# Row sums of ReLU on one core: the second load takes another 8 MB block in a different deal of rows to partitions, and the 15-row block comes third

## The chip, the core and the metric

The kernel runs on one core of a Trainium2 chip. The input lies in HBM, the chip's memory; DMA engines, 16 for the core, move it into SBUF, the core's working memory of 128 partitions. ScalarE (ACT) and VectorE (DVE) compute there; SyncE (SP) issues every DMA of this kernel. The metric is the device time of one execution in microseconds. Before the change the median of three runs is 161.04 us (160.92 to 161.04).

## The reference

```python
batch, seq, dim = 32, 512, 1024
x = randn(batch, seq, dim)          # float32, 64 MB

def reference(x):
    relu_x = np.maximum(x, 0)
    return np.sum(relu_x, axis=-1).astype(np.float32)
```

There are 16,384 rows of 1,024 numbers (4 KB each). Of each row the positive numbers are added up. The output is 64 KB.

## The kernel before

The input is seen as 16,384 rows. The first 2,048 rows, 8 MB, form block 0, and every further 2,048 rows another block: blocks 0 to 6 and a last one that is cut into smaller loads. A block holds 16 rows for each of the 128 partitions. There are three buffers `io0` to `io2` of 8 MB (`bufs`), used in turn.

*Which row lies where.* Block 0 is split. Its first 128 rows, one for each partition, are a load of their own of 512 KB (`ahead`), so that VectorE has something to add early. The other 1,920 rows are `xf`: 15 adjacent rows, 60 KB, for each partition. All later blocks are slices of `xv`, which gives each partition one long run of adjacent rows of the remaining input; of these a block takes 16 for each partition. The results lie in one SBUF tensor `res`, a column for each row of a partition (128 columns); column 0 stays unused, since the sums of the first 128 rows go through `one` and `turned`.

*The order of the loads.* The loop over j (lines 160 to 195) issues one 8 MB load per block, from SyncE, all on one queue. Load 0 is preceded by `ahead`. The first three have a buffer each and wait for nothing. A later one waits (`freed`) until VectorE has finished with the block that held its buffer three loads before. Counted with `ahead` the order of transfers is thus: 512 KB, then the 15-row load, then 16-row loads. The last 8 MB come as 8 rows, 4 rows and the last four rows in four unequal loads (lines 198 to 233), so that little work is left after the last byte.

*The work on a block.* `TWO[j]` lists how many rows one pair of instructions takes: ScalarE clamps them at zero in place (`clamp`, line 121), then VectorE adds up each row (`total`, line 129). `ACT[j]` and `DVE[j]` rows are done by a single instruction on one engine, which clamps and adds together (`act_row`, line 136; `dve_row`, line 144). The first three blocks are one pair of instructions each.

*The stores.* After all loads have been issued, SyncE issues the stores of the results (lines 237 to 240): columns 1 to 15 in two halves of 64 partitions, the first 128 sums, then columns 16 to 125 in one store that waits for nearly the last sum. The last two columns are stored at the very end (line 255).

Of the kernel before, what the change touches and what calls it, by code (L numbers as in the profile page):

```python
# [7 lines left out]
P = 128  # L8

ROWS = 16  # L10
NBUF = 3


TWO = [[15], [16], [16], [8, 8], [8, 8], [7, 7], []]
ACT = [0, 0, 0, 0, 0, 2, 9]
DVE = [0, 0, 0, 0, 0, 0, 7]

# [9 lines left out]
def kernel(tc: tile.TileContext, x: bass.AP, out: bass.AP):  # L27
    nc = tc.nc
    sems = Semaphores(tc)

    tc.close()
    tc.compile()
    nc.cur_bb = nc.bb_map[tc.start_bb_name]
    body = nc.cur_bb.bb.instructions
    ends = list(body)
    body.clear()
    n_stores = relu_sum(nc, sems, x, out)
    body.extend(ends)


    nc.cur_bb = nc.bb_map[tc.start_bb_name + "_end"]
    nc.cur_bb.bb.instructions.clear()
    nums = sorted(s.num for s in (*sems.loads, sems.act, sems.dve))
    cleared = range(nums[0], nums[-1] + 1)
    assert len(cleared) == len(nums)
    nc.sync.sem_clear(cleared)
    nc.sync.wait_ge(sems.stored, 16 * n_stores).then_inc(sems.stored, -16 * n_stores)
    open_without_barrier(tc, EARLY)


class Semaphores:
    def __init__(self, tc: tile.TileContext):
        n = 1 + len(TWO) + len(TAIL) + 2 + len(PIECES)
        self.loads = [tc.alloc_semaphore(f"load{i}") for i in range(n)]
        self.act = tc.alloc_semaphore("act")
        self.dve = tc.alloc_semaphore("dve")
        self.stored = tc.alloc_semaphore("stored")


def relu_sum(nc, sems: Semaphores, x: bass.AP, out: bass.AP):  # L60
    x_flat = x.flatten_outer_dims()
    N, D = x_flat.shape
    NT = N // P
    NB = len(TWO)
    assert N == P * NT == P * ROWS * (NB + 1)
    assert sum(TAIL) == ROWS - 4 and START_PIECE + END_PIECE + sum(PIECES) == D

    bufs = [nc.alloc_sbuf_tensor(f"io{i}", [P, ROWS, D], F32) for i in range(NBUF)]
    res = nc.alloc_sbuf_tensor("res", [P, NT], F32)
# [8 lines left out]
    one = nc.alloc_sbuf_tensor("one", [P, 32], F32)  # L78
    turned = nc.alloc_sbuf_tensor("turned", [P, 32], F32)
    N1 = P * ROWS  # L80
    xf = x_flat[P:N1].rearrange("(p m) d -> p m d", p=P)
    xv = x_flat[N1:].rearrange("(p m) d -> p m d", p=P)
    o_flat = out.rearrange("b s -> (b s)")
    oo = o_flat[:P].rearrange("(b i) -> b i", i=32)
    of = o_flat[P:N1].rearrange("(p m) -> p m", p=P)
    ov = o_flat[N1:].rearrange("(p m) -> p m", p=P)

    def rows(m, n):
        if m < ROWS:
            return xf[:, m - 1 : m - 1 + n, :]  # L90
        return xv[:, m - ROWS : m - ROWS + n, :]

    def sums(m, n, part):
        if m < ROWS:
            return of[part, m - 1 : m - 1 + n], res[part, m : m + n]
        return ov[:, m - ROWS : m - ROWS + n], res[:, m : m + n]

    n_load = n_act = n_dve = n_store = 0

    def load(dst, src, after=None):  # L100
        nonlocal n_load
        dma = nc.sync.dma_start(out=dst, in_=src)  # L102
        if after:
            dma.wait_op(sems.dve, after[1], "sem-ge")
        dma.then_inc(sems.loads[n_load], 16)
        n_load += 1
        return sems.loads[n_load - 1]

    def store(m, n, act, dve, part=slice(None)):
        nonlocal n_store  # L110
        dst, src = (oo, turned[0::32, :]) if m == 0 else sums(m, n, part)
        if act:
            nc.sync.wait_ge(sems.act, act)
        nc.sync.dma_start(out=dst, in_=src).wait_op(sems.dve, dve, "sem-ge").then_inc(
            sems.stored, 16
        )
        n_store += 1

    def clamp(ap, loaded):
        nonlocal n_act  # L120
        i = nc.scalar.activation(out=ap, in_=ap, func=RELU)  # L121
        if loaded is not None:
            i.wait_op(loaded, 16, "sem-ge")
        i.then_inc(sems.act, 1)
        n_act += 1

    def total(ap, m, n):
        nonlocal n_dve
        nc.vector.tensor_reduce(  # L129
            out=res[:, m : m + n], in_=ap, axis=mybir.AxisListType.X, op=ADD  # L130
        ).wait_op(sems.act, n_act, "sem-ge").then_inc(sems.dve, 1)
        n_dve += 1

    def act_row(ap, accum_out, loaded):
        nonlocal n_act
        i = nc.scalar.activation(out=ap, in_=ap, func=RELU, accum_out=accum_out)  # L136
        if loaded is not None:
            i.wait_op(loaded, 16, "sem-ge")
        i.then_inc(sems.act, 1)
        n_act += 1  # L140

    def dve_row(ap, accum_out, loaded):
        nonlocal n_dve
        i = nc.vector.tensor_scalar(  # L144
            out=ap,
            in0=ap,
            scalar1=0.0,
            scalar2=None,
            op0=MAX,
            op1=ADD,  # L150
            accum_out=accum_out,
        )
        if loaded is not None:
            i.wait_op(loaded, 16, "sem-ge")
        i.then_inc(sems.dve, 1)
        n_dve += 1

    freed = []
    m = 0
    for j in range(NB):  # L160
        buf = bufs[j % NBUF]
        c = 0
        if j == 0:
            ahead = load(buf[:, 0, :], x_flat[:P])
            c = 1
        loaded = load(
            buf[:, c:, :], rows(m + c, ROWS - c), j >= NBUF and freed[j - NBUF]
        )
        if j == 0:
            nc.vector.memset(one[:, :], 0.0).then_inc(sems.dve, 1)  # L170
            n_dve += 1
            nc.vector.wait_ge(sems.dve, n_dve)
            dve_row(buf[:, 0, :], one[:, 0:1], ahead)
            nc.vector.transpose(turned[:, :], one[:, :]).wait_op(  # L174
                sems.dve, n_dve, "sem-ge"
            ).then_inc(sems.dve, 1)
            n_dve += 1
            sums_ahead = n_act, n_dve
        act_waits = dve_waits = loaded
        for n in TWO[j]:  # L180
            clamp(buf[:, c : c + n, :], act_waits)
            total(buf[:, c : c + n, :], m + c, n)
            act_waits = None
            c += n
        for _ in range(ACT[j]):
            act_row(buf[:, c, :], res[:, m + c : m + c + 1], act_waits)
            act_waits = None
            c += 1
        for _ in range(DVE[j]):
            dve_row(buf[:, c, :], res[:, m + c : m + c + 1], dve_waits)  # L190
            dve_waits = None
            c += 1
        assert c == ROWS
        freed.append((n_act, n_dve))
        m += ROWS


    buf = bufs[NB % NBUF]
    c = 0
    for n in TAIL:  # L200
        loaded = load(
            buf[:, c : c + n, :], rows(m, n), None if c else freed[NB - NBUF]
        )
        for i in range(n):
            if i % 2 == 0 or (n == 8 and i == 7):
                act_row(buf[:, c, :], res[:, m : m + 1], loaded if i == 0 else None)
            else:
                dve_row(buf[:, c, :], res[:, m : m + 1], loaded if i == 1 else None)
            c += 1
            m += 1  # L210

    flat = buf[:, :, :].rearrange("p c d -> p (c d)")
    src = rows(m, 4).rearrange("p c d -> p (c d)")
    at = c * D
    split = 2 * D
# [4 lines left out]
    loaded = load(flat[:, at : at + b], src[:, :b])  # L220
    act_row(buf[:, c, :], res[:, m : m + 1], loaded)
    sums_act = n_act
    dve_row(buf[:, c + 1, :], res[:, m + 1 : m + 2], loaded)
    sums_dve = n_dve
    dve_row(flat[:, at + split : at + b], others[0], None)
    loaded = load(flat[:, at + end : at + 4 * D], src[:, end:])
# [7 lines left out]

    store(1, ROWS - 1, *freed[0], slice(0, P, 2))
    store(1, ROWS - 1, *freed[0], slice(1, P, 2))
    store(0, 1, *sums_ahead)
    store(ROWS, NT - ROWS - 2, sums_act, sums_dve)  # L240

    for i in range(len(PIECES) - 1):
        dve_row(parts[i][:, :], others[2 + i], arrived[i])
# [62 lines left out]
```

## Time and profile before

| | |
|---|---|
| median of three runs | 161.04 us (160.92 to 161.04) |
| the profiled execution | 160.93 us, of which the span from its first to its last instruction is 159.5 us |
| VectorE busy | 118.1 us (74%) |
| ScalarE busy | 103.4 us (65%) |
| read from HBM, written | 67.11 MB, 0.07 MB |
| mean rate over the span | 421 GB/s |
| loads issued | at 0.00 us (512 KB), 0.44 us (15 rows), 0.91 us and 1.38 us (16 rows); the next waits until 50.93 us |

The profile is one execution, with times in microseconds from its first instruction. Besides the groups of instructions it has a timeline, a list of waits, the chain of work that ended last, and a record of every DMA packet with its start, duration and size. The 64 KB packets, of which there are 768 in the six 16-row loads, take 2.418 us in the median; the 128 packets of 60 KB take 2.268 us. A duration of one instruction is the mean of its group. The two lines below are the clamps and the sums of the whole 16-row blocks; the columns are line, engine, operation, names, shapes and count, then busy time in us and mean of one in ns, then idle time in front of them and what ended it.

```profile
L129 DVE TENSOR_REDUCE res<-io 128x16 f32<-128x16384 f32 x2 | 34.4, 17220 | 6.2 <-ACT io L121 6.2
L121 ACT ACTIVATE io<-io 128x16384 f32<-128x16384 f32 x2 | 27.7, 13856 | 11.8 <-DMA io<-in_x_dram 11.8
```

### The profile page before, as it was taken

To read this page: it belongs to the slowest core of one execution; us is meant where nothing else is said; L and a number is where in the kernel's file an instruction comes from. 1 tells how busy PE (TensorE), PEld (TensorE's weight loads), DVE (VectorE), ACT (ScalarE), POOL (GpSimd) and SP (SyncE) were. 2 spreads that over 40 slices of the span, in tenths; PEclk is the share of its full clock that TensorE was granted. 3 is DMA by queue.
4 is the path that set the end of the run, shared out by engine and by line. 5 is a ranking of instruction groups with operands and counts; after the bars stand their busy time and mean duration, and the time that the engine had idled before them with its cause. 6 is when DMAs were issued, how large, how long until landed. Compare 5 with 4: busy or idle time off the path is not lost.

```text
span 159.5 us, 129 instructions
## 1 busy us (share of the span) xinstructions
DVE 118.1 (74%) x47; ACT 103.4 (65%) x50; POOL 0.2 (0%) x4
## 2 busy tenths in 40 slices
DVE  1200000029997299994999999999999999999986
ACT  3000059970799708996099951999329992499995
POOL 0000000000000000000000000000000000000000
DMA  9997996996996997998989969969969969899993
GB/s 378 493 401 339 493 526 263 526 526 263 526 509 279 526 460 329 526 411 378 526 362 427 526 263 526 526 263 526 526 263 526 509 279 526 345 444 390 410 415 116
DMA packets 2472, 67.18 MB, mean 421 GB/s; under 512 B 680, under 2 KB 936, under 8 KB 1192
## 3 DMA queue, kind: packets, MB, share of 16 engines
q1 hardware_dynamic: 2472, 67.18, 98.0%
HBM read 67.11 MB, written 0.07 MB: 421 GB/s over the span
## 4 chain that ended last, share of the span: by engine, by line
DMA 43%; DVE 34%; ACT 17%; another core or an unknown queue 3%; SPq 1%; issue 0%
DMA io<-in_x_dram 43%; DVE res L129 32%; ACT io L121 17%; DVE io L144 1%; SPq L102 1%; DVE piece L245 0%; DVE piece L144 0%
## 5 line engine op out<-in xcount | busy, mean ns | idle before, releaser
L129 DVE TENSOR_REDUCE res<-io 128x8 f32<-128x8192 f32 (+3 forms) x9 | 100.0, 11168 | 36.1 <-ACT io L121 36.1
L121 ACT ACTIVATE io<-io 128x8192 f32<-128x8192 f32 (+3 forms) x9 | 80.9, 9015 | 48.5 <-DMA io<-in_x_dram 48.5
L136 ACT ACTIVATE io<-io 128x1024 f32<-128x1024 f32 x20 | 20.9, 1045 | 6.0 <-DMA io<-in_x_dram 6.0
L144 DVE TENSOR_SCALAR_CACHE_REDUCE io<-io 128x1024 f32<-128x1024 f32 (+2 forms) x16 | 17.1, 1117 | 3.6 <-DMA io<-in_x_dram 3.5
L136 ACT ACTIVATION_READ_ACCUMULATOR io<-io 128x1 f32 x20 | 3.8, 188 | 0.0
L121 ACT ACT_TABLE_LOAD x1 | 1.3, 1283 | 0.1
L144 DVE DVE_READ_ACCUMULATOR io<-io 128x1 f32 x16 | 1.3, 82 | 0.0
L245 DVE TENSOR_SCALAR_CACHE_REDUCE piece<-piece 128x247 f32<-128x247 f32 x1 | 0.4, 410 | 0.0
L144 DVE TENSOR_SCALAR_CACHE_REDUCE piece<-piece 128x240 f32<-128x240 f32 x1 | 0.4, 404 | 0.0
L174 DVE STREAM_TRANSPOSE turned<-one 128x32 f32<-128x32 f32 x1 | 0.2, 211 | 0.0
L170 DVE MEMSET one<- 128x32 f32 x1 | 0.1, 85 | 0.1
L290 POOL MEMSET const-bfloat16-1.0<- 128x1 bf16 x1 | 0.1, 102 | 0.0
L290 POOL MEMSET const-uint8-127<- 128x1 uint8 x1 | 0.1, 102 | 0.0
L290 POOL MEMSET const-float32-0.0<- 128x1 f32 x1 | 0.1, 100 | 0.2 <-issue 0.2
L290 POOL MEMSET const-float32-1.0<- 128x1 f32 x1 | 0.1, 99 | 0.0
L144 DVE DVE_READ_ACCUMULATOR piece<-piece 128x1 f32 x1 | 0.1, 84 | 0.0
L245 DVE DVE_READ_ACCUMULATOR piece<-piece 128x1 f32 x1 | 0.1, 83 | 0.0
## 6 DMA issues: line engine op xcount, KB each, us to landing
io<-in_x_dram SPq DMA_DIRECT2D x1, 7680.0 KB, 21.3
io<-in_x_dram SPq DMA_DIRECT2D x1, 4096.0 KB, 21.6
io<-in_x_dram SPq DMA_DIRECT2D x1, 2048.0 KB, 26.1
io<-in_x_dram SPq DMA_DIRECT2D x1, 1164.0 KB, 28.4
io<-in_x_dram SPq DMA_DIRECT2D x1, 642.0 KB, 29.5
io<-in_x_dram SPq DMA_DIRECT2D x1, 512.0 KB, 3.3
piece<-in_x_dram SPq DMA_DIRECT2D x1, 122.0 KB, 29.2
piece<-in_x_dram SPq DMA_DIRECT2D x1, 120.0 KB, 29.4
```

The costliest lines, as they stand in the source:

```text
L102: dma = nc.sync.dma_start(out=dst, in_=src)
L121: i = nc.scalar.activation(out=ap, in_=ap, func=RELU)
L129: nc.vector.tensor_reduce(out=res[:, m : m + n], in_=ap, axis=mybir.AxisListType.X, op=ADD).wait_op(sems.act, n_act, "sem-ge").then_inc(se ...
L136: i = nc.scalar.activation(out=ap, in_=ap, func=RELU, accum_out=accum_out)
L144: i = nc.vector.tensor_scalar(out=ap, in0=ap, scalar1=0.0, scalar2=None, op0=MAX, op1=ADD, accum_out=accum_out,)
L170: nc.vector.memset(one[:, :], 0.0).then_inc(sems.dve, 1)
L174: nc.vector.transpose(turned[:, :], one[:, :]).wait_op(sems.dve, n_dve, "sem-ge").then_inc(sems.dve, 1)
L245: nc.vector.tensor_scalar(out=last[:, :], in0=last[:, :], scalar1=0.0, scalar2=None, op0=MAX, op1=ADD, accum_out=res[:, NT - 2 : NT - 1],) ...
L290: nc = _bacc.Bacc("TRN2", target_bir_lowering=False, num_devices=1)
```

## The change

The loop's first two blocks change places. Load 0 of the loop, the second load of the kernel, is now block 1, whole, 16 rows for each partition; the third load is the 15-row rest of block 0. `ahead` still is the first load, and goes to row 15 of the second buffer, where the 15-row load leaves room.

Block 1 is also dealt out in another way. Before, partition p took 16 rows of one long run. Now (`xs`) the block's 8 MB are seen as four parts of 2 MB (index j), each cut into 32 pieces of 64 KB (index g), and partition 4g+j takes piece g of part j. So partitions 0 to 3 begin 2 MB apart from each other, and partitions 0, 4, 8 ... begin 64 KB apart. The sums of this block go back in the same deal (`os`), by a store of their own; the columns from 32 on follow in the store that waits for nearly the last sum. Blocks 2 and up are as long runs as before, of an input that begins one block later.

```diff
-TWO = [[15], [16], [16], [8, 8], [8, 8], [7, 7], []]
+TWO = [[16], [15], [16], [8, 8], [8, 8], [7, 7], []]
...
-    xv = x_flat[N1:].rearrange("(p m) d -> p m d", p=P)
+    N2 = 2 * N1
+    xs = x_flat[N1:N2].rearrange("(j g m) d -> g j m d", g=32, j=4)
+    xv = x_flat[N2:].rearrange("(p m) d -> p m d", p=P)
...
-    ov = o_flat[N1:].rearrange("(p m) -> p m", p=P)
+    os = o_flat[N1:N2].rearrange("(j g m) -> g j m", g=32, j=4)
+    ov = o_flat[N2:].rearrange("(p m) -> p m", p=P)
...
-        return xv[:, m - ROWS : m - ROWS + n, :]
+        if m < 2 * ROWS:
+            return xs
+        return xv[:, m - 2 * ROWS : m - 2 * ROWS + n, :]
...
-        return ov[:, m - ROWS : m - ROWS + n], res[:, m : m + n]
+        if m < 2 * ROWS:
+            return os, res[:, m : m + n]
+        return ov[:, m - 2 * ROWS : m - 2 * ROWS + n], res[:, m : m + n]
...
     freed = []
-    m = 0
     for j in range(NB):
         buf = bufs[j % NBUF]
+        m = ROWS * (1 - j) if j < 2 else ROWS * j
         c = 0
+        n_rows = ROWS
         if j == 0:
-            ahead = load(buf[:, 0, :], x_flat[:P])
-            c = 1
-        loaded = load(
-            buf[:, c:, :], rows(m + c, ROWS - c), j >= NBUF and freed[j - NBUF]
-        )
-        if j == 0:
+            ahead = load(bufs[1][:, ROWS - 1, :], x_flat[:P])
             nc.vector.memset(one[:, :], 0.0).then_inc(sems.dve, 1)
             n_dve += 1
             nc.vector.wait_ge(sems.dve, n_dve)
-            dve_row(buf[:, 0, :], one[:, 0:1], ahead)
+            dve_row(bufs[1][:, ROWS - 1, :], one[:, 0:1], ahead)
             nc.vector.transpose(turned[:, :], one[:, :]).wait_op(
                 sems.dve, n_dve, "sem-ge"
             ).then_inc(sems.dve, 1)
             n_dve += 1
             sums_ahead = n_act, n_dve
+        if j == 1:
+            m = 1
+            n_rows = ROWS - 1
+        loaded = load(buf[:, :n_rows, :], rows(m, n_rows), j >= NBUF and freed[j - NBUF])
...
-        assert c == ROWS
+        assert c == n_rows
         freed.append((n_act, n_dve))
-        m += ROWS
+
+    m = ROWS * NB
...
-    store(1, ROWS - 1, *freed[0], slice(0, P, 2))
-    store(1, ROWS - 1, *freed[0], slice(1, P, 2))
+    store(1, ROWS - 1, *freed[1], slice(0, P, 2))
+    store(1, ROWS - 1, *freed[1], slice(1, P, 2))
     store(0, 1, *sums_ahead)
-    store(ROWS, NT - ROWS - 2, sums_act, sums_dve)
+    store(ROWS, ROWS, *freed[0])
+    store(2 * ROWS, NT - 2 * ROWS - 2, sums_act, sums_dve)
```

## The prediction

> **What bounds the kernel now.** I read the timeline of ScalarE first, because its first instruction on every block waits for that block's load. The columns are start, length, engine, line, operation, shapes, and in brackets the idle time before it with its releaser.
>
> ```profile
> 21.71 13.00 ACT L121 ACTIVATE io<-io 128x15360 f32<-128x15360 f32 x1 [20.32 <-DMA io<-in_x_dram]
> 41.06 13.86 ACT L121 ACTIVATE io<-io 128x16384 f32<-128x16384 f32 x1 [6.34 <-DMA io<-in_x_dram]
> 60.42 13.86 ACT L121 ACTIVATE io<-io 128x16384 f32<-128x16384 f32 x1 [5.50 <-DMA io<-in_x_dram]
> 79.77 13.95 ACT L121 ACTIVATE io<-io 128x8192 f32<-128x8192 f32 x2 [5.49 <-DMA io<-in_x_dram]
> ```
>
> Every start waits for a transfer, and the blocks arrive 19.35 us apart, 8.39 MB each: 433.5 GB/s. Next the DMA part of the page, for whether the transfers ever pause.
>
> ```profile
> q1 hardware_dynamic: 2472, 67.18, 98.0%
> ```
>
> The 16 DMA engines are busy for 98.0% of the span. Last the chain of waits, for the end.
>
> ```profile
> 126.77 28.43 DMA io<-in_x_dram
> 155.20 0.02 issue
> 155.22 2.02 DVE io L144 x6
> 157.25 0.35 DVE piece L144 x2
> 157.59 0.02 issue
> 157.62 0.42 DVE piece L245 x2
> ```
>
> A transfer ends it and 2.8 us of unbroken VectorE work follow. The chain's 51.6 us of VectorE before 126.77 do not bind: the transfer issued there sends its first packet at 136.9, behind the block before it. So the end is the start of the stream, plus the bytes at the engines' rate, plus this fixed tail.
>
> The trace's DMA packet records say where the stream is not at its rate. One packet is one partition's part of a load; each engine carries eight per load and then a 4-byte packet that counts the load.
>
> ```
> load             packet     last engine's count   mean of 16    spread
> ahead, 512 KB    4 KB        2.966                 2.715         0.416
> 15 rows         60 KB       21.371                20.995         0.574
> 16 rows         64 KB       40.692                40.329         0.572
> 16 rows         64 KB       60.033                59.672         0.577
> ```
>
> From one packet's start to the next, an undisturbed engine takes 2.2635 us for 60 KB and 2.414 us for 64 KB. The third load takes 19.334 us on average, against 8 x 2.414 + 0.006 = 19.318: nothing is lost. The second should take 8 x 2.2635 + 0.006 = 18.115; it takes 18.280 on average and 18.405 on the engine that is last (21.371 - 2.966). So it loses 0.165 us on average and 0.290 on the engine that sets the end. Nearly all of it is in each engine's first three packets, before 10 us; the worst single packet took 2.746 instead of 2.267, 0.479 too much. The engine that is last here stays last, so these 0.290 us are carried to the end.
>
> **The change part by part.** *Bytes:* the same 67.11 MB. The second load grows by one row, 19.318 - 18.115 = 1.203 us, and the third shrinks by that. At the engines' rate the fourth load begins when it began: 0.
>
> *Addresses of the second load.* Partition 4g+j now reads from j x 2 MB + g x 64 KB. Groups of four partitions begin 64 KB apart, where the 15-row block has 4 x 60 = 240 KB and the other blocks 256 KB. What this does to the 0.290 us no row shows; it can be bounded. Below: it vanishes, a gain of 0.29. Above: the last engine gets the worst packet twice, 2 x 0.479 = 0.96, a loss of 0.67. The nearest rows disagree about the cause: the third load goes from the one spacing to the other without loss, so neither spacing as such costs anything; the loss belongs to the first 10 us, when all engines begin together. Then another spacing leaves most of it. I take 0.21 us on the last engine, between the mean engine's 0.165 and 0.290: a gain of **0.08 us**. What a gain can be at most is the important number: 0.29 us, 0.18%.
>
> *Compute.* The first large clamp starts 1.20 - 0.08 later, at 22.83 instead of 21.71, and takes 13.86 instead of 13.00; its sums end at 22.83 + 13.86 + 0.04 + 17.22 = 53.95 instead of 50.90. The load that refills this buffer is issued that much later. It has cover: the first load needed 1.03 us from issue to first packet, so packets come at 55.0, and the first engine to run out of queued work does so at 59.46. If the cover of 4.4 us were gone, each us later would show in full. The 15-row block then starts at about 40.98, is clamped by 53.98, summed by 70.15 (72.17 before), so the next refill is issued 2.0 us earlier. At 74.31 VectorE takes up the third block as before. Cost on the path: 0.
>
> *Row 0 of the first load* goes to the second buffer. Its row sum at 3.35 is long over when the 15-row load ends; nothing else reads that row until its load at 70: 0.
>
> *Stores.* One is added, 128 pieces of 64 B; the last but one shrinks from 440 B to 376 B a partition. SyncE issues it after 130.7, when it waits until 156.48 anyway; one issue takes 0.35 to 0.6 us. Its eight packets per engine, at the 11 to 15 ns of the 60 B store's, are 0.1 us, behind the last load's and before the 376 B store's, which begin at 157.32; the short stores end at 157.04 now. Hidden: 0; without that gap 0.1 us.
>
> *Issue of the second load.* SyncE needs 0.43 us for it at 0.44; the first engine is free for it at 2.56. Were the less regular source twice as dear, it would still be in time: 0.
>
> Sum: 160.93 us (the profiled execution, span 159.5 and 1.43 around it) - 0.08 = **160.85 us**. The median shown is 161.04, 0.11 above this execution.
>
> A rule speaks against the change. The Trainium skill (DMA: Bandwidth & Descriptors, "Latency and other measured facts") reports that row pitches at large powers of two slow copies between HBM tensors: 207 of 214 GB/s at 512 KiB, 164 at 2 MiB. Successive partitions are now 2 MB apart; by that rule this load would be an estimated 19.3 x (214/164 - 1) = 5.9 us longer and the time 166.8. No row of this trace has such a pitch; I do not follow the rule, since the sixteen streams in flight together are here 64 KB apart and the 2 MB steps come one after another.
>
> **The rivals.** *The loss vanishes.* For it: 0.290 us are there, in this load, in the first 10 us; with 64 KB between the groups the starting points are all different. Against: they are different now too. Time: 160.93 - 0.29 = 160.64, or up to 160.72 with 0.08 left.
>
> *The streams collide.* The closest streams in the trace are those of the load ahead, 16 KB apart. Its engine that ends last takes 1.442 us for eight packets that undisturbed take 8 x 0.1555 = 1.244: 16% too much. At 64 KB the second load may behave so. If it settles after two packets of 0.479 too much each, the time is 160.93 - 0.29 + 0.96 = 161.60; if the 16% lasts for the load, 3.1 us, it is 163.7. Against: the load ahead is itself smooth after its first two or three packets. It decides, as slower than the median by 0.2% (161.36), from a loss of 0.72 us on the last engine, 0.09 us a packet.
>
> *The load is not dealt as the change says.* The source's slowest dimension is now 32 and not 128; the engines might share the load otherwise, unevenly. No row shows such a load. If it keeps only eight engines busy at a time it doubles, 160.93 + 19.3 = 180.2; smaller unevenness costs anything below.
>
> The Trainium skill's rule in the same page ("Why a DMA increments its semaphore by 16 and not by 1") takes the largest number up to 16 that divides the slowest dimension of both sides, which would be 16 for 32 and 128; by it this rival costs 0.
>
> **How the numbers follow.** Within 0.2% of the median shown (160.72 to 161.36), which is about what a measurement of this kernel can tell from no change: the forecast, 0.50, with its own range 160.74 to 161.12 (0.10 to 0.48 us left on the last engine). The loss vanishes: 0.24, faster. The streams collide: 0.18, slower, just under half of it below 161.8. Dealt otherwise: 0.08, slower, nearly all above. The range 160.6 to 161.8 leaves out about 0.18 above and 0.02 below.
>
> **What would show it.** The first 128x16384 clamp at 22.8 (22.6: loss gone; above 23.3: collision), the next one at 40.9 to 41.1, and 19.35 us between all later ones; in the packet records of the second load, eight 64 KB packets an engine, at 2.418 us after the first three. Packets above 2.45 throughout mean collision; engines with other than eight packets, another deal. The prediction is wrong as well if a gap opens in the queue near 59.5, or if the tail's VectorE work waits for the added store.

## The result, and the profile after

The changed kernel takes 163.20 us (163.15 to 163.54) against 161.03 us before, a ratio of 1.0142 (95% interval 1.0129 to 1.0154). That is slower, above the predicted range. The profiled execution takes 163.54 us, 2.61 more than that of before; its span is 162.1 us.

The timeline of ScalarE after the change (start, length, engine, line, operation, shapes, idle time and its releaser):

```profile
25.54 13.86 ACT L128 ACTIVATE io<-io 128x16384 f32<-128x16384 f32 x1 [24.14 <-DMA io<-in_x_dram]
43.69 13.00 ACT L128 ACTIVATE io<-io 128x15360 f32<-128x15360 f32 x1 [4.29 <-DMA io<-in_x_dram]
63.04 13.86 ACT L128 ACTIVATE io<-io 128x16384 f32<-128x16384 f32 x1 [6.35 <-DMA io<-in_x_dram]
82.40 13.95 ACT L128 ACTIVATE io<-io 128x8192 f32<-128x8192 f32 x2 [5.50 <-DMA io<-in_x_dram]
```

The first block comes at 25.54, where 22.83 was expected. The third clamp stands at 63.04 instead of 60.42, 2.62 later, and from there on the blocks again come about 19.35 us apart. So all of the loss lies in the second load, and nothing is made up or lost after it. The end of the chain of waits confirms that:

```profile
129.39 28.45 DMA io<-in_x_dram
157.84 0.02 issue
157.87 1.98 DVE io L151 x6
159.85 0.34 DVE piece L151 x2
160.19 0.02 issue
160.21 0.42 DVE piece L254 x2
```

It is the chain of before, 2.65 us later (157.87 against 155.22). The start of that chain has SyncE's issue of the second load (SPq; start, length), here before the change and after it:

```profile
0.44 0.42 SPq L102
```

```profile
0.44 0.67 SPq L109
```

On the page the queue is a little emptier, 97.2% against 98.0%:

```profile
q1 hardware_dynamic: 2616, 67.18, 97.2%
```

The packet records say where in the load the time goes. "Loss" is the last engine's count of this load, less that of the load before, less the undisturbed 18.115 us (15 rows) or 19.318 us (16 rows).

```
                      before (15 rows)     after (16 rows, dealt)
load before counted   2.550 to 2.966       2.613 to 2.937
first packets begin   2.556 to 2.972       2.636 to 4.437
longest first packet  2.746                3.935
longest second        2.548                3.316
packets 3 to 8        2.267 (max 2.404)    2.418 (max 2.420)
last engine's count   21.371               25.194
loss                  0.29                 2.94
```

Two things are new. Nine of the sixteen engines begin the dealt load only after the last engine has finished what lay before it, the last of them 1.5 us after. And every engine's first packet takes 0.3 to 1.5 us too long, on the engines that began in time too; on the eight that began first the second packet is 0.2 to 0.9 us too long as well. From the third packet on the load runs at full rate, without any exception. Of the 2.94 us the load lost 0.29 before, so 2.65 are new, close to the 2.61 by which the profiled times differ.

### The profile page after: what moved, and what is told of

Same layout as the page of the kernel before. It is cut to its first block, busy times and chain, and to the rows that moved or that the text cites. A ratio compares the mean times of both kernels' runs of the same rounds, so it can differ in the third digit from the quotient of the medians.

```text
span 162.1 us, 131 instructions
## 1 busy us (share of the span) xinstructions
DVE 118.0 (73%) x47; ACT 103.4 (64%) x50; POOL 0.2 (0%) x4
## 3 DMA queue, kind: packets, MB, share of 16 engines
q1 hardware_dynamic: 2616, 67.18, 97.2%
## 4 chain that ended last, share of the span: by engine, by line
DMA 44%; DVE 34%; ACT 17%; another core or an unknown queue 4%; SPq 1%; issue 0%
DMA io<-in_x_dram 44%; DVE res L136 32%; ACT io L128 17%; DVE io L151 1%; SPq L109 1%; DVE piece L254 0%; DVE piece L151 0%
```

## The experiments

I had thought of the addresses: streams 64 KB apart that get in each other's way ("collision"). The late beginnings suggested another cause: that the descriptors of this load (the orders that tell an engine which bytes to move) reach the engines late ("late descriptors"). A third theory put it down to the order of the loads.

**The deal undone.**

```diff
-    xs = x_flat[N1:N2].rearrange("(j g m) d -> g j m d", g=32, j=4)
+    xs = x_flat[N1:N2].rearrange("(p m) d -> p m d", p=P)
```

The output side `os` follows it.

> The changed kernel with the deal of the second load undone: order, sizes and the added store stay, but partition p takes the p-th 64 KB of the 8 MB block, so groups of four partitions begin 256 KB apart. Theory 'collision' (streams that begin 64 KB apart meet at the start, until they are spread in time): 161.0 us, the second load's last engine loses 0.7 us at most. Theory 'late descriptors' (the source of three dimensions is handed out to the engines late, up to 1.5 us): also 161.0. Theory 'order' (a first big load of 64 KB packets or the 15-row block third is what costs): 163.2.

Measured: 161.23 us (160.93 to 161.69), ratio 1.0011 (1.0000 to 1.0021). First packets begin from 2.621 to 3.188, the longest takes 2.767, the loss is 0.06 us. The 512 KB load ended 0.22 us later than before (3.182 against 2.966), so the big load ends at 22.560, where the one of before would have ended with one row more (21.371 + 1.203 = 22.574). From the second block on ScalarE's starts are those of before:

```profile
22.90 13.86 ACT L128 ACTIVATE io<-io 128x16384 f32<-128x16384 f32 x1 [21.50 <-DMA io<-in_x_dram]
41.04 13.00 ACT L128 ACTIVATE io<-io 128x15360 f32<-128x15360 f32 x1 [4.29 <-DMA io<-in_x_dram]
60.39 13.86 ACT L128 ACTIVATE io<-io 128x16384 f32<-128x16384 f32 x1 [6.35 <-DMA io<-in_x_dram]
```

Order, sizes, buffers and the added store cost next to nothing; the theory of the order falls. It is the deal.

**The deal at other distances.** First the kernel before with its 15-row load dealt, so that groups lie 60 KB apart (the output side `of` follows):

```diff
-    xf = x_flat[P:N1].rearrange("(p m) d -> p m d", p=P)
+    xf = x_flat[P:N1].rearrange("(j g m) d -> g j m d", g=32, j=4)
```

> The kernel before, with only the deal: the 15-row block stays second, but is dealt in four parts, partition 4g+j takes 60 KB at j x 1,920 KB + g x 60 KB, so groups begin 60 KB apart. 'Collision' at multiples of 64 KB: 60 KB apart the streams begin 4 KB off each other in that measure, and the load loses 0.3 us at most: 160.7 to 161.1. 'Late descriptors': the source has three dimensions as in the change, first packets begin up to 1.5 us late: 162.3 or more. 'Order': 161.0.

Measured: 162.72 us (161.65 to 163.74), ratio 1.0108 (1.0068 to 1.0148). First packets begin as late as 4.324, the longest takes 3.249, the loss is 1.94 us. Then the changed kernel with `g=64, j=2`, 128 KB apart:

> The changed kernel with the second load dealt in two parts of 4 MB and 64 pieces: partition 2g+j, groups of four partitions begin 128 KB apart, the source still has three dimensions. 'Collision': less than at 64 KB if the meeting weakens with distance, 161.3 to 162.5; the first two packets of an engine longer than 2.418 us, the rest not. 'Late descriptors': first packets begin as late as in the changed kernel (up to 4.4 us) and the time is 162.5 to 163.2.

Measured: 163.64 us (163.42 to 163.94), ratio 1.0160 (1.0145 to 1.0175). First packets as late as 4.904, loss 2.88 us: not less than at 64 KB. Third, addresses nearly as in the undone deal, but with a source of three dimensions that can't be joined to two:

```diff
-    xs = x_flat[N1:N2].rearrange("(j g m) d -> g j m d", g=32, j=4)
+    xs = x_flat[N1 : N1 + 32 * 65].rearrange("(g r) d -> g r d", r=65)
+    xs = xs[:, :64, :].rearrange("g (j m) d -> g j m d", j=4)
```

> The changed kernel, whose second load has a source of the same three dimensions (32 x 4 x 64 KB) but nearly the addresses of the undone deal: the four partitions of a group take adjacent runs of 64 KB, groups are 260 KB apart. It reads rows other than it should there, so these sums are not the reference's; size and time of the load are. Theory 'late descriptors' (a source of three dimensions is handed to the engines late and in pieces, wherever it points): 162.7 to 163.6, first packets begin as late as 4.4 us. Theory 'collision at the start' (near streams meet when all begin together): 161.2, as with the deal undone, first packets begin by 3.2 us.

Measured: 163.44 us in the median; the four executions took 161.50, 163.44, 163.44 and 163.77. The profiled one is the fastest of them. In it first packets begin in time (2.697 to 2.985), two of the sixteen take 3.026 and 3.236, and the loss is 0.78 us. So at a distance of 260 KB three executions of four were as slow as the changed kernel; where these three lost it no profile shows.

**The distance without the deal.** The 8 MB block as four plain 2 MB loads, in each of which groups lie 64 KB apart:

```diff
-    xs = x_flat[N1:N2].rearrange("(j g m) d -> g j m d", g=32, j=4)
+    xs = x_flat[N1:N2].rearrange("(j p m) d -> j p m d", p=P, j=4)
...
-        loaded = load(buf[:, :n_rows, :], rows(m, n_rows), j >= NBUF and freed[j - NBUF])
+        if j == 0:
+            for i in range(4):
+                loaded = load(buf[:, 4 * i : 4 * i + 4, :], xs[i])
+                if i < 3:
+                    nc.scalar.wait_ge(loaded, 16)
+        else:
+            loaded = load(buf[:, :n_rows, :], rows(m, n_rows), j >= NBUF and freed[j - NBUF])
```

The output side `os` follows it.

> The changed kernel with the 8 MB block as four plain loads of 2 MB, 4 rows (16 KB) a partition: groups of four partitions begin 64 KB apart, as in the change, with a source of two dimensions. 'Late descriptors': 161.0 to 161.5, the four loads lose 0.7 us at most on the last engine. 'Collision at the start': the engines have to spread in time here too, they lose 1.0 to 2.5 us: 162.2 to 163.5.

Measured: 162.05 us (161.91 to 162.07), outside what "late descriptors" allowed, yet not by the load. The four loads end at 22.674, 19.620 us after the load before; undisturbed, 4 x 4.862 = 19.448 (the distance of the later ones among them). They lose 0.17 us. The rest is at the very end, in the instruction that waits for the last piece:

```profile
158.72 0.41 DVE L260 TENSOR_SCALAR_CACHE_REDUCE piece<-piece 128x247 f32<-128x247 f32 x1 [0.93 <-DMA piece<-in_x_dram]
```

Its idle time, 0.93 us, was none before. This kernel's store of the block has 512 pieces of 16 B, queued behind that last piece; that these hold up its count is a guess that wasn't tried by itself. The 0.17 us speak against "collision": 64 KB apart in plain loads costs less than the 0.29 us that the start cost before. The packets are 16 KB here, though, not 64 KB.

**The deal later.** The kernel before, with the same dealt block (`xs`, and its store, as in the change) loaded fourth:

```diff
+        m = ROWS * (3 - j) if j in (1, 2) else ROWS * j
```

> The kernel before, with block 1 dealt as in the change but loaded fourth, when its descriptors are queued some 40 us ahead and the engines run 0.57 us apart. 'Collision': the engines must still spread to about 2.1 us, so the last one loses 1.0 to 2.0 us in this load: 162.0 to 163.0. 'Late descriptors': 161.0, no loss in the fourth load. A theory that only the common start matters: 161.0 as well.

Measured: 161.03 us (160.96 to 161.56), ratio 1.0002 (0.9992 to 1.0011). The dealt load goes from the last count 40.639 to 59.968, a loss of 0.01 us. Addresses, distance and shape are those of the change, and cost nothing here, with the load issued some 39 us before its first packet is due.

**More work ahead of the dealt load.** Four of the 15 rows go first, as a load of their own (the other 11 follow the dealt load):

```diff
             ahead = load(bufs[1][:, ROWS - 1, :], x_flat[:P])
+            first = load(bufs[1][:, :4, :], rows(1, 4))
```

> The changed kernel with 2 MB of the 15-row load moved ahead of the dealt load: 4.8 us more work for every engine before the dealt load's first packet is needed, which then is at 7.5 us instead of 2.7. 'Late descriptors' (last engine served at 4.4 us, first packets 1.5 us too long): the engines have work meanwhile, loss below 0.5 us, 161.0 to 161.4. 'Collision at the start': the engines are still within 0.6 us of each other and must spread to 2 us: 162.0 to 163.2.

Measured: 162.30 us (162.09 to 162.81). The dealt load is clean: first packets begin from 7.559 to 8.122, the longest takes 2.451, the loss is 0.02 us. With that "collision" falls: the addresses are those of the change, all engines begin within 0.57 us, and nothing is lost. What the kernel loses is somewhere else, so that its total lies in the range of "collision" by coincidence:

```profile
27.83 26.75 ACT L128 ACTIVATE io<-io 128x16384 f32<-128x16384 f32 x2 [26.43 <-DMA io<-in_x_dram]
```

```profile
41.72 50.40 DVE res L136 x3
```

The first is the timeline, the second the chain of waits from 50 to 90 us. The first block comes 4.9 us later, and VectorE works without a break from 41.72. So the buffer is refilled late: that load is issued at 58.97, and needs its first packet at 59.57. The load behind goes from the last count 60.079 to 80.758, 1.36 us too long. That is the cover the prediction had worked out, and here it is used up. The same with one row, and with two:

> The changed kernel with one of the 15 rows (512 KB) as a load of its own ahead of the dealt load: 1.2 us more work for each engine, while the dealt load is issued 0.47 us later, net 0.74 us more cover (2 MB removed the whole loss of the dealt load). 'Late by the clock' (the dealt load's last engine gets its descriptors about 3.3 us after the issue is done): last first packet about 4.9 us with a need at 4.2, loss on the last engine between 0.7 and 2.2: 161.5 to 162.5. 'Late after the load before' (the hand-out waits for the engine's earlier load, however long that is): starts up to 1.5 us after the need, as in the changed kernel: 162.7 to 163.5.

> The same with two rows (1 MB) ahead of the dealt load, net 1.95 us more cover. 'Late by the clock': all 16 engines have their descriptors when they need them (5.1 us and later), no loss beyond 0.5 us: 160.9 to 161.4. 'Late after the load before': 162.7 to 163.5.

Measured: 162.06 us (161.89 to 162.24) and 161.55 us (161.27 to 161.70), the second 0.15 above what "late by the clock" allowed. With one row the last engine has lost 1.22 us by the dealt load's end, 0.7 of it already in the plain one-row load. Here no engine waits for the dealt load: its first packets begin within 0.04 us of the end of the work before. Yet nine of them take 3.6 to 3.9 us, so packets can be long without being late. With two rows the dealt load's first packets all take 2.418 and it loses nothing; 0.46 us are lost in the two-row load ahead of it. Counted from the end of the first 512 KB, loss falls as work ahead grows: 2.94, 1.22, 0.46 and 0.18 us with 0, 512 KB, 1 MB and 2 MB more. Whether a plain 8 MB load would make these short loads lose as much wasn't run.

**The dealt load first, and its plain counterpart.**

```diff
+            loaded = load(buf[:, :, :], rows(m, ROWS))
             ahead = load(bufs[1][:, ROWS - 1, :], x_flat[:P])
...
-        loaded = load(buf[:, :n_rows, :], rows(m, n_rows), j >= NBUF and freed[j - NBUF])
+        if j > 0:
+            loaded = load(buf[:, :n_rows, :], rows(m, n_rows), j >= NBUF and freed[j - NBUF])
```

> The changed kernel with the dealt 8 MB load first on the queue and the 512 KB load second, so that nothing hides when the dealt load's packets begin. A plain first load has its first packets on the 16 engines from 1.03 to 1.52 us. 'Late descriptors': first packets begin over 2 to 3 us, the last at about 4.0 us (4.44 in the changed kernel, where the issue was 0.44 later); nothing covers it: 164 to 165. 'Collision at the start': they begin by 1.6 us and are long: 162 to 163.

> The counterpart of the kernel with the dealt load first: the same order with the deal undone, plain 64 KB packets from the start. 'Late descriptors': first packets begin from 1.03 to 1.52 us and take 2.42 to 2.8 us, 160.7 to 161.1, so that the dealt load first costs 0.8 to 1.2 us. 'Cold start' (any first big packets are 1 us long): first packets 3.1 to 3.7 us as with the dealt load, 161.8.

Measured: dealt 161.89 us (161.78 to 161.95), plain 161.25 us (161.17 to 161.47). Dealt, fifteen first packets begin from 1.455 to 1.877 and one at 2.510; plain, they begin from 1.013 to 1.967. The longest first packets take 3.689 and 3.392. So first big packets on idle engines are up to about 1 us too long whatever the deal. The deal costs 0.64 us here: less than the 0.8 to 1.2 of "late descriptors", more than the nothing of "cold start". With nothing ahead of it the dealt load's first packets begin only some 0.5 us after the plain one's, the last at 2.510, and "late descriptors" in its simple form (the last at 4.0) falls.

**The issue alone.** The kernel before, with only the second load kept off the shortened form of the issue (`dge_precook`):

```diff
+        nc.dge_precook = j != 0
         loaded = load(
             buf[:, c:, :], rows(m + c, ROWS - c), j >= NBUF and freed[j - NBUF]
         )
+        nc.dge_precook = True
```

> The kernel before, same addresses, sizes and order; only the way its second load (15 rows, a source of two dimensions) is issued differs: it is kept off the shortened issue that the assembler marks for plain 128-partition loads, and which the dealt load did not get either. Theory 'slow issue' (what is late is any load that SyncE must work out in full): issue 0.67 instead of 0.43 us, first packets late or long, 162 to 163.5. Theory 'three dimensions' (handing out a source of 32 x 4 pieces is what takes long): issue 0.67 us or less, loss as before, 160.9 to 161.3.

Measured: ten executions from 161.06 to 163.45 us, median 161.62, ratio 1.0050 (1.0013 to 1.0086), between the two expectations. SyncE needs 0.574 us for the issue instead of 0.425 (0.666 for the dealt load). Two executions took 163.4, as long as the changed kernel; the profiled one, 161.09, shows no late packet. Nothing but the form of the issue differs, so the long form is enough to lose 2.4 us now and then. That they are lost in the second load isn't shown, since no profile caught such an execution.

**The next loads held back.**

```diff
-rows(m, n_rows), j >= NBUF and freed[j - NBUF])
+rows(m, n_rows), sums_ahead if j == 1 else j >= NBUF and freed[j - NBUF])
```

> The changed kernel, with the two loads behind the dealt one held back until the first row sums are turned (about 4.8 us), so that nothing else is handed out while the dealt load is; its 19.3 us of work cover the wait. Theory 'the next loads get in the way of the handing out': first packets by 3.2 us and 2.4 to 2.7 us long, 161.0 to 161.6. Theory 'the dealt load alone is slow to hand out': as the changed kernel, 162.7 to 163.5.

Measured: 163.03 us (161.72 to 163.92). First packets begin as late as 5.006, the loss is 2.80 us. What is issued behind the dealt load is not what makes it late.

With this one there are five kernels with a dealt load right behind the 512 KB on SyncE's queue. Of their 21 executions 18 took 162.68 us or more, the other three 161.50 to 161.72. With three dimensions the time is lost nearly always.

**The load before on another queue.** The 512 KB are issued by ScalarE:

```diff
-        dma = nc.sync.dma_start(out=dst, in_=src)
+        dma = by.dma_start(out=dst, in_=src)
...
-            ahead = load(bufs[1][:, ROWS - 1, :], x_flat[:P])
+            ahead = load(bufs[1][:, ROWS - 1, :], x_flat[:P], by=nc.scalar)
```

> The changed kernel with the first 512 KB issued by ScalarE on its own queue, so that the dealt load is the first of SyncE's queue and waits behind nothing there. 'Late by the clock': as with the dealt load first, packets begin from 1.4 to 2.5 us, 161.5 to 162.2. 'Late after the load before, in one queue': also gone, 161.2 to 162.2. If the dealt load's packets begin up to 4.4 us here too, neither queue nor order makes them late, but any work on the engines while it is handed out: 162.5 to 163.5.

Measured: 161.28 us (161.00 to 161.91), ratio 1.0015 (1.0005 to 1.0025). The dealt load's packets begin from 2.797 to 2.974, the longest takes 2.624, the loss is 0.31 us, and the load ends at 22.596, with the deal undone at 22.560. The timeline of this kernel:

```profile
0.00 1.83 SPq L109 DMA_DIRECT2D io<-in_x_dram  x3
0.12 0.36 ACTq L109 DMA_DIRECT2D io<-in_x_dram  x1
22.94 13.86 ACT L128 ACTIVATE io<-io 128x16384 f32<-128x16384 f32 x1 [21.14 <-DMA io<-in_x_dram]
158.59 0.41 DVE L254 TENSOR_SCALAR_CACHE_REDUCE piece<-piece 128x247 f32<-128x247 f32 x1 [0.48 <-DMA piece<-in_x_dram]
```

With the same 512 KB ahead, the same addresses and the same shape the block is there at 22.94, not 25.54. Two things differ at once, though: the queue, and the dealt load's issue, which begins at 0.00 instead of 0.44. The last line is a wait of 0.48 us for the last piece, which accounts for part of this execution's 161.91.

## Why the prediction was wrong

*What bounds the kernel*: right. The end moved with the stream, 2.62 us at the third clamp, 2.65 at the end.

*Issue of the second load*: this is the step that failed. It priced the less regular source by SyncE's time, "were the less regular source twice as dear, it would still be in time: 0". SyncE's time was 0.666 us, less than twice as dear, and yet the load began late and slowly: first packets up to 1.5 us after the need, and long first and second packets, 2.94 us on the last engine in place of 0.21. The issue ended at 1.10 us, and the last engine began at 4.437, idle for 1.5 us. The runs show when it happens: with a load that SyncE issues in the long form, behind another one on the same queue, with only 512 KB ahead (nearly always with three dimensions, now and then with two). Undo the deal (0.06 us), issue the load before from ScalarE (0.31), put 2 MB ahead (0.02) or load the block fourth (0.01), and the big load loses about as little as before (0.29) or less. Why such a load begins so, the runs leave open.

*Addresses of the second load*: the term of 0.21 us, bounded by 0.96, measured 2.94, and not because of the addresses. In the one profile of the kernel with the deal undone the loss was 0.06, but the load before ended later by nearly as much, and the kernel didn't gain. The text also had the distance in the other blocks wrong: in the kernel before their partitions lie 112 rows apart, so groups are 4 x 448 = 1,792 KB apart, not 256. The conclusion drawn from the distances, that no spacing costs anything by itself, held: loads with groups 64 KB (0.01 us, loaded fourth), 256 KB (0.06) and 1,792 KB apart all run at full rate.

*The rivals*: "the streams collide" gave 161.6 to 163.7 us and the right place, the first two packets, with the wrong cause: that 163.20 lies in its range, and that its sign (a first clamp above 23.3) came, is luck. "Not dealt as the change says" looked at the three dimensions, but for the share of each engine; in the trace of the changed kernel all sixteen carry eight 64 KB packets of the load, as the Trainium skill's rule on the number of engines has it (DMA: Bandwidth & Descriptors, "Why a DMA increments its semaphore by 16 and not by 1"). No rival had a load that comes late.

*The rule on large powers of two* that I didn't follow (the same page, "Latency and other measured facts") doesn't show here: with partitions 2 MB apart packets three to eight take 2.418 us in the changed kernel, the rate of every other block, and loaded fourth the same block loses 0.01 us. Which of its partitions were in flight together the traces don't show.

*Compute and refill*: right. The refill was issued at 56.68 with a need at 60.49, so nothing was added; in the kernel with four rows ahead the cover was used up.

*Stores*: priced at 0, and in the changed kernel's profile nothing waits for them. Other kernels with the added store waited for the last piece in their profiled execution (0.23 us with the block loaded fourth, 0.32 with the deal undone, 0.48 with two queues), and some didn't; the one profile of before has no such wait. That the store is the cause wasn't tried.

What stays open is the mechanism. If the long form were late by the clock alone, the two-queue kernel, whose dealt load is issued 0.44 us earlier, should by estimate still have had its last first packet at 4.44 - 0.44 = 4.0 us with a need at 2.97, 1 us late; it had it at 2.974. If it waited for the end of the load before, more work ahead shouldn't help. And lateness doesn't explain the long packets: with one row ahead nothing began late, nine packets were long all the same, and part of the loss fell on the plain load ahead. No profile here shows the handing out of a load to the engines itself.

## What to carry to other kernels

A load whose source has more dimensions is not only a different set of addresses; it may be issued in another way, and here its packets began later and ran slower than the issuing instruction suggests. In this kernel such a load was clean with 1 to 2 MB more queued ahead of it, and cost about 2 us right behind a short first load on the same queue. But moving work ahead has a price of its own (161.55 and 162.30 us in all); of the kernels with the deal only the one that loads the block fourth had the time of before (161.03). Price a start-up step by the first packets on all 16 engines: here the engine that was last at the start was still last at the end of the stream.

## What the runs showed that I had not expected

With the long form the time of the same program varied: 161.06 to 163.45 us over ten executions with it, 160.83 to 161.67 over the nineteen of the kernel before beside them. And engines that begin with 64 KB packets from idle take 2.59 to 3.39 us for the first one instead of 2.418, even for a plain load; that kernel is only 0.2 us slower in all (161.25 against 161.07).
